# Dilated convolution on one core: two input loads are moved behind output stores, and all transfers go whole

## The chip, the cores and the metric

The kernel runs on one core of a Trainium2 chip. The core has a matrix engine (TensorE, PE in the profile), a vector engine (VectorE, DVE), a scalar engine (ScalarE, ACT), GpSimd (POOL) and SyncE (SP). In this kernel SP computes nothing: it issues every DMA, the transfers between HBM and the on-chip memory SBUF. The metric is the device time of one execution in microseconds (us). The profile is of one execution; its span runs from the first to the last instruction.

## The reference

A 3x3 convolution with dilation 2 and padding 2 over 16 images of 64 channels and 64 x 64 pixels, to 128 output channels:

```python
batch, c_in, h, w, c_out, k, dilation = 16, 64, 64, 64, 128, 3, 2
for b in range(batch):
    for co in range(c_out):
        for ci in range(c_in):
            for kh in range(k):
                for kw in range(k):
                    output[b, co] += weight[co, ci, kh, kw] * x_pad[b, ci, kh*dilation:kh*dilation+h, kw*dilation:kw*dilation+w]
```

Input and output are float32. The input is 16.8 MB, the output 33.6 MB, so two bytes are stored for each byte that is loaded.

## The kernel before

**Pairs and groups.** Two images share the 128 partitions (64 channels each), which makes 8 pairs, 0 to 7. Each pair is worked in 4 groups of 16 output rows, so that the main loop runs over 32 groups G = 0 to 31; pair 0 is G 0 to 3, pair 6 is G 24 to 27, pair 7 is G 28 to 31.

**One group.** PE makes three sums in PSUM: psP from the row sums xs, then psA and psB from the f16 input. psP has one buffer, psA and psB share three. ACT copies psP to SBUF (p_sb, L261). DVE adds p_sb to psA and to psB and writes the result into the output ring osb (L268). The next group's psP cannot be started before ACT has copied the last one out.

**Input.** A pair is loaded as float32 into one of three x32 buffers (L65, in the function load) and then cast to f16 in four chunks by ACT (L83) or POOL (L85). The f16 tiles have four buffers. Which chunk is cast in which group stands in a table, CASTS; chunk c belongs to pair c // 4. In group G, ACT runs the p_sb copy first and the casts of the table behind it. The entries that matter here are these:

```python
12: ((24, A), (25, A)),
13: ((26, A), (27, A)),
16: ((28, A), (29, A)),
17: ((30, A), (31, A)),
```

Chunks 24 to 27 are pair 6 and are needed by the matmuls from G = 24 on; chunks 28 to 31 are pair 7 and are needed from G = 28 on. ACT runs its instructions in the order of the program.

**Output.** The ring osb holds the outputs of three pairs (12.6 MB). Pair 3 writes the place of pair 0, pair 4 that of pair 1, and so on.

**The order of the transfers.** All DMAs are issued by SP, in the order of the program; the schedule is written by hand. Before the loop come the weights, pair 0 in two parts, pair 1 and pair 2. Pairs 3, 4 and 5 are loaded at the ends of G = 0, 2 and 3, when an x32 buffer comes free. At G = 5 and 6 the table MIXED issues pairs 6 and 7 in halves of 1 MB, each half followed by a half of one image of pair 0 (half_load, L223, and store, L206). From G = 7 on each pair is stored when its last group is done: pairs 1 and 2 in halves of images, pairs 3 to 6 as whole images of 2 MB. The last pair is stored twice, after its second and its fourth group. In all SP issues 38 DMAs.

Of the kernel before, what the change touches and what calls it, by code (L numbers as in the profile page):

```python
# [10 lines left out]
def kernel(  # L11
# [7 lines left out]
    nc = tc.nc  # L19

    B, CI, H, W = x.shape
# [7 lines left out]
    P = 128  # L29
    f32 = mybir.dt.float32  # L30
# [4 lines left out]
    HW = H * W  # L35
    GR = 16
    NG = H // GR
# [9 lines left out]
    fpool = ctx.enter_context(tc.tile_pool(name="fpool", bufs=XF))  # L47
# [7 lines left out]
    x_pair = x.rearrange("(nb two) c h w -> nb (two c) (h w)", two=2)  # L55
# [4 lines left out]
    x32_tiles, x16_tiles, xs_tiles = {}, {}, {}  # L60

    def load(pb, cuts=(0, H)):
        x32_tiles[pb] = fpool.tile([P, HW], f32, tag="x32", name="x32")
        for lo, hi in zip(cuts[:-1], cuts[1:]):
            nc.sync.dma_start(  # L65
                out=x32_tiles[pb][:, lo * W : hi * W], in_=x_pair[pb, :, lo * W : hi * W]
            )
# [3 lines left out]
    def o_pair(pb):  # L71
        at = pb % OB * 2 * HW
        return o_ring[:, at : at + 2 * HW]
# [13 lines left out]
    def rowsum(c):  # L87
        pb, g = divmod(c, NG)
        if g == 0:
            xs_tiles[pb] = sxpool.tile([P, HW // 2], f16, tag="xs", name="xs")  # L90
        v = x16_tiles[pb][:, g * GR * W : (g + 1) * GR * W].rearrange(
            "p (b e q) -> p b e q", e=2, q=2 * W
        )
        s = xs_tiles[pb][:, g * NH : (g + 1) * NH].rearrange("p (b q) -> p b q", q=2 * W)
        nc.vector.tensor_tensor(out=s, in0=v[:, :, 0], in1=v[:, :, 1], op=add)  # L95
# [33 lines left out]
    def turn(k):  # L129
# [24 lines left out]
        out=x16_tiles[0][:, 8 * W : 18 * W], in_=x32_tiles[0][:, 8 * W : 18 * W]  # L154
# [23 lines left out]
    def casts(G):  # L178
        for c, eng in CASTS.get(G, ()):
            cast(c, eng)  # L180

    def product(ps, src, kind, blk0, nblk, first, last):
        for j in (1, 0, 2):
            dw = (j - 1) * d
            o0, o1 = max(0, -dw), W - max(0, dw)
            t = kind * KW + j
            for hb in range(2):
                pp = slice(hb * CI, (hb + 1) * CI)
                rhs = src(pp, dw + o0, dw + o1)
                po = ps[:, hb * NH + blk0 * 2 * W : hb * NH + (blk0 + nblk) * 2 * W]  # L190
                po = po.rearrange("p (r w) -> p r w", w=W)[:, :, o0:o1]
                nc.tensor.matmul(  # L192
                    out=po,
                    lhsT=w_sb[pp, t * CO : (t + 1) * CO],
                    rhs=rhs,
                    start=first and j == 1,
                    stop=last and j == 2,
                )

    def blocks(x16, b0, n, e):  # L200
        v = x16.rearrange("p (b e r w) -> p b e r w", e=2, r=2, w=W)
        return lambda pp, c0, c1: v[pp, b0 : b0 + n, e, :, c0:c1]

    def store(pb, m, r0=0, r1=H, rows=((0, P),)):
        for lo, hi in rows:
            nc.sync.dma_start(  # L206
                out=out_img[2 * pb + m, lo:hi, r0 * W : r1 * W],
                in_=o_pair(pb)[lo:hi, m * HW + r0 * W : m * HW + r1 * W],
            )

    def pair_store(pb):
        cuts = (0, H // 2, H) if pb < 3 else (0, H)
        for lo, hi in zip(cuts[:-1], cuts[1:]):
            for m in range(2):
                store(pb, m, lo, hi)

    LOADS = {0: (3,), 2: (4,), 3: (5,)}

    def half_load(pb, k):
        if k == 0:  # L220
            x32_tiles[pb] = fpool.tile([P, HW], f32, tag="x32", name="x32")
        r = slice(k * HW // 2, (k + 1) * HW // 2)
        nc.sync.dma_start(out=x32_tiles[pb][:, r], in_=x_pair[pb, :, r])  # L223

    MIXED = {5: ((6, 0, 0, 0), (6, 1, 0, 1)), 6: ((7, 0, 1, 0), (7, 1, 1, 1))}
    FOUR = ((0, P - 4), (P - 4, P))
    ROWS4 = 8

    for G in range(ngroups):
        pb, g = divmod(G, NG)  # L230
        x16 = x16_tiles[pb]
        xs = xs_tiles[pb].rearrange("p (r w) -> p r w", w=W)
        o = o_pair(pb).rearrange("p (m b e q) -> p m b e q", m=2, e=2, q=2 * W)
        b0 = g * NBLK

        def summed():
            ps = ppool.tile([P, 2 * NH], f32, tag="p", name="psP")
            sv = lambda pp, c0, c1: xs[pp, g * GR // 2 : (g + 1) * GR // 2, c0:c1]
            product(ps, sv, 0, 0, NBLK, True, True)
            return ps  # L240

        if G:
            psP = summed()

        psA = apool.tile([P, 2 * NH], f32, tag="ab", name="psA")
        product(psA, blocks(x16, b0, NBLK, 1), 1, 0, NBLK, True, False)
        z = 1 if g == 0 else 0
        product(psA, blocks(x16, b0 + z - 1, NBLK - z, 1), 2, z, NBLK - z, False, True)

        psB = apool.tile([P, 2 * NH], f32, tag="ab", name="psB")  # L250
        product(psB, blocks(x16, b0, NBLK, 0), 3, 0, NBLK, True, False)
        z = 1 if g == NG - 1 else 0
        product(psB, blocks(x16, b0 + 1, NBLK - z, 0), 4, 0, NBLK - z, False, True)

        if not G:
            psP = summed()

        if not G:
            casts(0)
        p_sb = spool.tile([P, 2 * NH], f32, tag="psb", name="p_sb")  # L260
        nc.scalar.copy(out=p_sb, in_=psP)  # L261
        if G:
            casts(G)
        if G + 1 < ngroups:
            rowsum(G + 1)
        pv = p_sb.rearrange("p (m b q) -> p m b q", m=2, q=2 * W)
        for e, ps in ((0, psA), (1, psB)):
            nc.vector.tensor_tensor(  # L268
                out=o[:, :, b0 : b0 + NBLK, e],
                in0=ps.rearrange("p (m b q) -> p m b q", m=2, q=2 * W),  # L270
                in1=pv,
                op=add,
            )

        for q in LOADS.get(G, ()):
            load(q)
        for q, k, h, m in MIXED.get(G, ()):
            half_load(q, k)
            store(0, m, h * H // 2, (h + 1) * H // 2)
        if G <= 6:  # L280
            continue
        if pb == npairs - 1:
            if g % 2 == 1:
                store(pb, 0, (g - 1) * GR, (g + 1) * GR)
                if g == 1:
                    store(pb, 1, 0, 2 * GR - ROWS4)
                    store(pb, 1, 2 * GR - ROWS4, 2 * GR, FOUR)
                else:
                    store(pb, 1, (g - 1) * GR, (g + 1) * GR)
        elif g == NG - 1:  # L290
            pair_store(pb)

# [33 lines left out]
```

## Time and profile before

| what | value |
|---|---|
| time, median of 3 runs (lowest to highest) | 127.23 us (127.01 to 127.34) |
| the profiled execution: time, span | 126.86 us, 125.0 us |
| PE busy | 104.9 us (84%) |
| DVE busy | 92.7 us (74%) |
| ACT busy | 58.7 us (47%) |
| HBM read and written | 17.07 MB, 33.55 MB |
| mean DMA rate over the span | 406 GB/s |

The time is 1.86 us more than the span, which is what lies outside the first and the last instruction. A DMA has two times in the trace: when SP issues it, and when it lands, that is when its completion reaches the waiting engine. The time from issue to landing holds the wait behind everything that was issued before it. In the rows of the timeline the first number is the start, the second the length from the first start to the last end, both in us, and xN the number of instructions merged into the row. In the rows of the stretches (windows) the line gives the stretch, then the busy time and the count of each engine, the granted PE clock, the busy share of the DMA engines and GB/s.

### The profile page before, as it was taken

What the parts mean: (1) busy time and instruction counts of PE and PEld (TensorE: products, weight loads), DVE (VectorE), ACT (ScalarE), POOL (GpSimd) and SP (SyncE); (2) the same over time, 40 slices, a digit from 0 to 9 for tenths busy, and PEclk for the clock granted to TensorE, in tenths of its full rate; (3) what the DMA queues carried; (4) which work ended last, traced back from release to release, by engine and by line L of the source; (5) the groups of instructions that cost most, each with busy time, mean ns of one, the idle gap of its engine ahead of it and who ended that gap; (6) DMA issues with size and microseconds to landing.
All of it is one profiled execution on the core that took longest, in us unless ns stands there. A gap on an engine that the chain in (4) does not pass through costs nothing.

```text
span 125.0 us, 2358 instructions
## 1 busy us (share of the span) xinstructions
PE 104.9 (84%) x1000; PEld 55.2 (44%) x1000; DVE 92.7 (74%) x103; ACT 58.7 (47%) x61; POOL 9.6 (8%) x15
## 2 busy tenths in 40 slices
PE   6876999999999999999999999999999999800000
PEld 2343444555555555555555555555555555300000
DVE  0752998989998889879988898889888988720000
ACT  4375876798569437943794333333333333300000
POOL 2402305124200000000000000000000000000000
PEclk9999999999999999999999999999999999996555
DMA  4999999999999999999999999999999999999991
GB/s 128 376 428 445 430 430 435 419 425 425 390 375 422 422 432 422 427 419 419 425 432 427 414 443 435 430 425 430 440 425 419 430 435 425 435 409 415 428 383 68
DMA packets 5330, 50.78 MB, mean 406 GB/s; under 512 B 584, under 2 KB 584, under 8 KB 1096
## 3 DMA queue, kind: packets, MB, share of 16 engines
q1 hardware_dynamic: 5320, 50.63, 96.7%
q8 instruction: 8, 0.13, 0.4%
q14 instruction: 2, 0.02, 0.0%
HBM read 17.07 MB, written 33.55 MB: 405 GB/s over the span
## 4 chain that ended last, share of the span: by engine, by line
PE 69%; DVE 1%; DVEq 1%; issue 0%
PE psA L192 28%; PE psB L192 27%; PE psP L192 14%; DVE osb L268 1%; DVEq L324 1%; DVEq L268 0%
## 5 line engine op out<-in xcount | busy, mean ns | idle before, releaser
L192 PEld LDWEIGHTS <-w_sb 64*128 64x128 f16 x960 | 53.3, 94 | 48.8 <-issue 2.0
L261 ACT COPY p_sb<-psP 128x1024 f32<-128x1024 f32 x32 | 32.4, 1012 | 41.0 <-PE psP L192 39.1
L268 DVE TENSOR_TENSOR osb<-psA,p_sb 128x1024 f32<-128x1024 f32 x32 | 39.1, 1223 | 12.5 <-PE psA L192 6.1
L192 PE MATMUL psA<-x,w_sb 64*128 64x496 f16 (+3 forms) x384 | 45.0, 365 | 0.8 <-ACT x L156 0.8
L192 PE MATMUL psB<-x,w_sb 64*128 64x496 f16 (+3 forms) x384 | 45.0, 365 | 0.0
L268 DVE TENSOR_TENSOR osb<-psB,p_sb 128x1024 f32<-128x1024 f32 x32 | 39.0, 1219 | 0.0
L192 PE MATMUL psP<-xs,w_sb 64*128 64x496 f16 (+1 forms) x192 | 26.0, 371 | 1.7 <-ACT p_sb L261 1.5
L83 ACT CAST x<-x 128x1024 f16<-128x1024 f32 (+2 forms) x24 | 24.3, 1051 | 3.4 <-DMA x<-in_x_dram 3.4
L95 DVE TENSOR_TENSOR xs<-x 128x512 f16<-128x512 f16 x32 | 15.6, 488 | 0.7 <-ACT x L83 0.7
L85 POOL CAST x<-x 128x896 f16<-128x896 f32 (+2 forms) x7 | 7.4, 1067 | 19.3 <-DMA x<-in_x_dram 19.3
L111 PE MATMUL dm<-zero 128*128 128x512 f16 x10 | 4.1, 532 | 1.2 <-DVE zero L103 1.2
L121 DVE CAST wd<-w 128x192 f16<-128x192 f32 x1 | 0.5, 499 | 2.6 <-DMA w<-in_weight_dram 2.6
L111 PEld LDWEIGHTS <-zero 128*128 128x128 f16 x10 | 1.0, 121 | 2.6 <-DVE zero L103 1.2
L134 PEld LDWEIGHTS <-wd 128*64 128x64 f16 x30 | 0.9, 109 | 1.9 <-DVE wd L121 1.3
L134 PE MATMUL wt<-ident,wd 128*64 128x128 f16 x30 | 1.4, 224 | 0.4 <-DVE wd L121 0.4
L123 ACT ACT_TABLE_LOAD x1 | 1.3, 1283 | 0.7 <-PEq L310 0.7
L123 ACT CAST wd<-w 128x192 f16<-128x192 f32 x1 | 0.5, 542 | 1.7 <-DMA w<-in_weight_dram 1.7
L146 ACT CAST w_sb<-wt 128x384 f16<-128x384 f32 x1 | 0.5, 479 | 1.2 <-PE wt L134 1.2
L156 ACT CAST x<-x 128x512 f16<-128x512 f32 x1 | 0.6, 617 | 0.8 <-DMA x<-in_x_dram 0.8
L122 POOL TENSOR_TENSOR wd<-w 128x192 f16<-128x192 f32 x1 | 0.8, 794 | 2.5 <-DMA w<-in_weight_dram 2.5
L153 DVE CAST x<-x 128x640 f16<-128x640 f32 x1 | 0.5, 494 | 0.6 <-DMA x<-in_x_dram 0.6
L103 DVE MEMSET zero<- 128x256 uint32 x1 | 0.3, 272 | 0.9 <-PEq L310 0.9
(12 smaller groups left out, 4.6 us busy)
## 6 DMA issues: line engine op xcount, KB each, us to landing
out_dram<-osb SPq DMA_DIRECT2D x8, 2048.0 KB, 17.9
out_dram<-osb SPq DMA_DIRECT2D x15, 1024.0 KB, 19.6
x<-in_x_dram SPq DMA_DIRECT2D x5, 2048.0 KB, 13.1
x<-in_x_dram SPq DMA_DIRECT2D x4, 1024.0 KB, 15.9
x<-in_x_dram SPq DMA_DIRECT2D x1, 1088.0 KB, 5.6
x<-in_x_dram SPq DMA_DIRECT2D x1, 960.0 KB
out_dram<-osb SPq DMA_DIRECT2D x1, 768.0 KB, 14.8
w<-in_weight_dram SPq DMA_DIRECT2D x1, 288.0 KB, 3.0
```

Source lines behind the costliest of these rows:

```text
L83: eng.copy(out=out, in_=in_)
L85: eng.tensor_copy(out=out, in_=in_)
L95: nc.vector.tensor_tensor(out=s, in0=v[:, :, 0], in1=v[:, :, 1], op=add)
L111: nc.tensor.matmul(out=dm[:, 0:512], lhsT=zero[:, 0:P], rhs=zero)
L122: nc.gpsimd.tensor_tensor(out=wdv[:, 3], in0=wv[:, 0], in1=wv[:, 1], op=sub)
L123: nc.scalar.copy(out=wdv[:, 2], in_=wv[:, 0])
L134: nc.tensor.matmul(out=wts[k % 3][r * CI : (r + 1) * CI, c0 + j * CO : c0 + (j + 1) * CO], lhsT=wd[:, t * CI : (t + 1) * CI], rhs=ident,)
L156: nc.scalar.copy(out=x16_tiles[0][:, 0 : 8 * W], in_=x32_tiles[0][:, 0 : 8 * W])
L192: nc.tensor.matmul(out=po, lhsT=w_sb[pp, t * CO : (t + 1) * CO], rhs=rhs, start=first and j == 1, stop=last and j == 2,)
L261: nc.scalar.copy(out=p_sb, in_=psP)
L268: nc.vector.tensor_tensor(out=o[:, :, b0 : b0 + NBLK, e], in0=ps.rearrange("p (m b q) -> p m b q", m=2, q=2 * W), in1=pv, op=add,)
L324: with _tile.TileContext(nc) as tc:
```

## The change

Pairs 6 and 7 are no longer loaded in halves between the stores of pair 0. They become entries of the table LOADS, at G = 7 and G = 11, and pairs 1 and 2 are stored ahead of that load in their last group. Pair 0 is stored at the end of G = 3, behind the load of pair 5. All stores of pairs 0 to 6 are of whole images. The table CASTS is as it was.

```diff
     def pair_store(pb):
-        cuts = (0, H // 2, H) if pb < 3 else (0, H)
-        for lo, hi in zip(cuts[:-1], cuts[1:]):
-            for m in range(2):
-                store(pb, m, lo, hi)
-
-    LOADS = {0: (3,), 2: (4,), 3: (5,)}
-
-    def half_load(pb, k):
-        if k == 0:
-            x32_tiles[pb] = fpool.tile([P, HW], f32, tag="x32", name="x32")
-        r = slice(k * HW // 2, (k + 1) * HW // 2)
-        nc.sync.dma_start(out=x32_tiles[pb][:, r], in_=x_pair[pb, :, r])
-
-    MIXED = {5: ((6, 0, 0, 0), (6, 1, 0, 1)), 6: ((7, 0, 1, 0), (7, 1, 1, 1))}
+        for m in range(2):
+            store(pb, m)
+
+    LOADS = {0: (3,), 2: (4,), 3: (5,), 7: (6,), 11: (7,)}
...
+        later = pb in (1, 2)
+        if g == NG - 1 and later:
+            pair_store(pb)
         for q in LOADS.get(G, ()):
             load(q)
-        for q, k, h, m in MIXED.get(G, ()):
-            half_load(q, k)
-            store(0, m, h * H // 2, (h + 1) * H // 2)
-        if G <= 6:
-            continue
         if pb == npairs - 1:
...
-        elif g == NG - 1:
+        elif g == NG - 1 and not later:
             pair_store(pb)
```

The order in SP's queue is then: weights, pairs 0 to 5, two images of pair 0, two of pair 1, load of pair 6, two images of pair 2, load of pair 7, and from there on stores alone, 30 DMAs in all.

## The prediction

> **What bounds the kernel now.** I read the page's header and slices first, to see which resource is never idle.
>
> ```profile
> span 125.0 us, 2358 instructions
> PE   6876999999999999999999999999999999800000
> DMA  4999999999999999999999999999999999999991
> ```
>
> Each digit is a fortieth of the span. PE is full up to about 109 us and then has nothing to do; the DMA engines are full from 3 us to the end. So two things run side by side: 50.63 MB through the queue, and 32 groups on PE. The end is the queue's. PE's own end matters only if it moves far enough to let the queue run dry.
>
> Next the stretches, for the rate of the queue and the clock (the last three columns are granted clock, DMA share, GB/s).
>
> ```profile
> 34.50:41.00 6.50, 6.50 (x66) 3.57 (x64) 6.01 (x8) 5.62 (x6) 0.00 (x0) 1.00 0.98 397
> 38.30:56.00 17.70, 17.70 (x174) 9.55 (x171) 15.10 (x18) 11.71 (x13) 0.00 (x0) 1.00 1.01 425
> 60.00:100.00 40.00, 40.00 (x394) 21.81 (x390) 35.66 (x40) 16.94 (x17) 0.00 (x0) 1.00 1.01 429
> 112.00:113.00 1.00, 0.00 (x0) 0.00 (x0) 0.00 (x0) 0.00 (x0) 0.00 (x0) 1.00 0.95 401
> 113.00:114.00 1.00, 0.00 (x0) 0.00 (x0) 0.00 (x0) 0.00 (x0) 0.00 (x0) 0.72 0.96 408
> ```
>
> A mixed queue (38 to 56 us) and a queue of stores (60 to 100 us) move at 425 and 429 GB/s. At 427 a transfer of 2.097 MB takes 4.9 us.
>
> Then the DMA issues, one at a time: issue time from SP's timeline, and size and time to landing from the list of issues.
>
> ```profile
> 23.07 0.33 SPq L65 DMA_DIRECT2D x<-in_x_dram  x1
> x<-in_x_dram SPq DMA_DIRECT2D x1, 2048.0 KB, 11.4
> 28.76 0.33 SPq L223 DMA_DIRECT2D x<-in_x_dram  x1
> x<-in_x_dram SPq DMA_DIRECT2D x1, 1024.0 KB, 9.5
> x<-in_x_dram SPq DMA_DIRECT2D x1, 1024.0 KB, 19.9
> ```
>
> Pair 5 is issued at 23.07 and lands at 34.5. The first half of pair 6 lands at 28.76 + 9.5 = 38.3. The last row is the second half of pair 7, issued at about 33.1 and landed at 53.0: three half stores and three half loads were issued between pair 5 and it, and it came behind all of them. A load waits for the stores issued before it; the queue serves in order of issue.
>
> Last, the timeline around the casts of pairs 6 and 7.
>
> ```profile
> 48.65 2.10 ACT L83 CAST x<-x 128x1152 f16<-128x1152 f32 x2
> 50.75 1.01 ACT L261 COPY p_sb<-psP 128x1024 f32<-128x1024 f32 x1
> 53.03 0.81 PE L192 MATMUL psP<-xs,w_sb 64*128 64x512 f16 x6
> ...
> 61.02 2.10 ACT L83 CAST x<-x 128x1152 f16<-128x1152 f32 x2
> 63.12 1.01 ACT L261 COPY p_sb<-psP 128x1024 f32<-128x1024 f32 x1
> 65.40 0.81 PE L192 MATMUL psP<-xs,w_sb 64*128 64x512 f16 x6
> ```
>
> At 48.65 (G = 12) ACT casts pair 6, and behind it, in ACT's order, stands the p_sb copy of G = 13, which PE needs to start psP of G = 14 at 53.03. At 61.02 (G = 16) it is the same with pair 7, the copy of G = 17, and psP of G = 18 at 65.40. Before the change both pairs have landed by then (latest 53.0).
>
> **The change part by part.** The sum runs against the profiled execution: 126.86 us, of which 125.0 is span and 1.86 lies outside; the median is 0.37 higher.
>
> *Whole transfers.* Twelve half stores become six, four half loads two: 38 DMAs become 30. Bytes stay. Eight issues of 0.34 us go from SP, which lies idle. In the queue, halves land 2.45 us apart (38.3 to 53.0 is six of them), 2 x 2.45 = 4.9, as a whole one takes; so I take nothing. The bounds are 0 and the one place where halves were slow: from 34.5 to 40.74 (the first half store's landing, 29.14 + 11.6) two halves took 6.2 instead of 4.9 us, 1.3 lost as the queue went from loads to stores.
>
> *Pair 0's stores* leave at about 24.5 us, when the group's second add ends (23.23 + 1.22), instead of at 29 to 35, behind pair 5 in the queue; the order of service stays gapless, since pair 1's first store, issued at 38.29 before, can go by then at the latest, and pair 0's 4.19 MB keep the queue busy until 34.5 + 9.8 = 44.3 or later. The first group of pair 3, which overwrites pair 0's place, writes at 48.86; pair 0 has landed by 45.6 at the latest. No new wait there. SP's 22.2 us of waits on landings (11.5 on stores, 10.7 on loads) mostly vanish, worth nothing as the queue was full under them.
>
> *Pair 6's load* is moved behind four images (8.39 MB). From pair 5's landing: 34.5 + 5 x 4.9 = 59.0, or 60.3 if the turn from loads to stores costs 1.3 again. I take 60.3, since the nearest row is that same turn; the two ends are kept. ACT wants it at 48.65, so ACT stands still for 11.7 us. Queued behind on ACT is the copy of G = 13: 60.3 + 2.1 (two casts) = 62.4, copied by 63.4, psP of G = 14 starts at 63.4 instead of 53.0. PE is 10.4 us late. DVE follows, its adds need p_sb; it is busy 2.93 of 3.10 us per group (two adds of 1.22 and a row sum of 0.49), so it wins nothing back.
>
> *Pair 7's load* stands behind two more images: 60.3 + 3 x 4.9 = 75.0 (73.7 without the turn). The queue is full up to there: pair 2 is complete at G = 11, before any delay (about 48.5). ACT comes to G = 16's casts at 61.02 + 10.4 = 71.4 and waits 3.6 us: casts to 77.1, copy of G = 17 to 78.1, psP of G = 18 at 78.1 instead of 65.4. PE is 12.7 us late in total; this second wait contains the first, so 12.7 depends on 75.0 alone.
>
> *The end.* From G = 18 on nothing is loaded and the queue lives on what PE delivers. Pair 3's stores go at 60.77 + 10.4 = 71.2, and behind pair 7 they land at 75.0 + 9.8 = 84.8. Pair 4's go at 73.14 + 12.7 = 85.8: the queue is dry. A cold start costs 2.3 us beyond the bytes: the weights, 0.295 MB, were issued at 0.73 and used at 3.74, 3.0 us less 0.7 for bytes. Pair 4 lands at 85.8 + 2.3 + 9.8 = 97.9, pair 5, issued at 98.2, at 110.3, pair 6 is issued at 97.88 + 12.7 = 110.6, dry again. From there 8.39 MB are left (pairs 6 and 7): 110.6 + 2.3 + 19.6 = 132.5. Pair 7's last stores, issued at 110.25 + 12.7 = 123.0, are queued in time. The tail after the last landing is 1.0 us (124.0 to 125.0 now). Span 133.5, time 135.4; against the median 135.7.
>
> In short: time is about 122.7 + delay above a delay of 4.1 us, from the profile's 126.86 with the span's 125.0 as floor, since below that the queue doesn't run dry.
>
> One page speaks for a longer time: the Trainium skill, "DMA: Bandwidth & Descriptors", section "Specifications", gives an HBM limit per core of about 358 GB/s, below the 435 of the fabric. By it, as an estimate, a whole transfer takes 5.9 us, pair 7 lands 8 x 0.96 = 7.7 us later, the last 8.39 MB take 3.8 us more, and the time is near 147. This trace disagrees: 429 GB/s over 40 us.
>
> **The rivals.**
>
> *Loads don't wait for stores* (faster). If reads overtook queued writes, pair 6 would land soon after its issue at 38 us and pair 7 after its at 49 us, ahead of 48.65 and 61.02; no wait arises, the end stays the queue's, and at best the turn's 1.3 us are saved: 127.2 - 1.3 = 125.9. It decides from the point where the delay falls under 4.1 us, that is where pair 7 lands before 66.4. Against it stands the landing at 53.0 of a load issued at 33.1. 0.04.
>
> *The wait is hidden* (same, 127.2): the same threshold, reached by part of that overtaking. With bytes in order, the queue would have to move 16.8 MB from 34.5 to 66.4, 526 GB/s; no slice of the page shows over 445. 0.03.
>
> *Every turn costs* (slower still). After the change the queue turns three times more (stores to pair 6, to stores, to pair 7). At 1.3 each pair 7 lands at 78.9 and the time is 139.6. For: the turn at 34.5. Against: the alternating halves after it ran at 425 GB/s. 0.10.
>
> *The clock falls* (slower a little). PE stops at 108.9 and its granted clock is 1.00 up to 113 and 0.50 by 114, so some 4.5 us of idling. The first wait (10.4 us) is longer, the second (PE idle 2.3 us) shorter. After the first wait PE starts slow; the six opening dummies took 457 ns each from 1.18 us, the two at 4.59 took 300, so the slow start lasts at most 3.4 us and costs at most 1.7. The second wait, 2.3 us long, hides that. If the clock falls there too, 1.7 show: 137.4. 0.08. The Trainium skill, "TensorE: Matmul & The Clock Gate", part 1, has it that one idle window of about 3.4 us halves the clock and about 3.4 us of work restores it; by that the second wait wouldn't, and the sum stays.
>
> **How the numbers follow.** The forecast as computed has 0.75: 135.7. Its lower end is no turn loss (134.4) with the fastest slice's 445 GB/s (eight transfers 0.19 us shorter each), 132.9. Its upper end takes the clock's 137.4 and a second turn. The range of 133 to 138.5 leaves out the overtaking and hidden cases (0.07) and most of the turns (0.08). A measurement can tell about 0.3% (0.4 us) from no change. Faster 0.04, same 0.03, slower 0.93.
>
> **What would show it.** Right: ACT's waits on input grow from 3.4 us to about 19, one of 11.7 at 48.7 and one of 3.6 at 71.4; PE has holes before G = 14 and G = 18; the DMA slices fall under 9 from about 85 us on; GB/s is unchanged before. Wrong: pair 6 landing before 54 us, or DMA slices full to the end in spite of PE's holes, which would mean that the queue had more in store than I count.

## The result

The changed kernel takes 138.01 us, median of 6 runs (137.52 to 138.16), against 127.28 us of the kernel before in 6 runs. The ratio is 1.082, with a 95% interval from 1.0766 to 1.0873. The forecast was 135.7 us, range 133.0 to 138.5. The profiled execution took 138.06 us, with a span of 136.2 us.

**The page after.** The header and slices of the changed kernel:

```profile
span 136.2 us, 2343 instructions
PE   6896998999999996003999989999999999980000
PEclk9999999999999999955599999999999999999555
DMA  4999999999999999999996996399479929999981
```

PE has a hole in slices 16 to 19 (it stands still from 53.3 to 63.5 us), and its granted clock falls in it. The DMA slices are full until about 72 us and have holes from there to the end: the queue, which was the bound, now runs out of work.

**Who waits.** Lines of the changed kernel's list of waits (engine, line, releaser; us in total, times, longest):

```profile
DVE osb L258 <- ACT p_sb L251: 20.0, 11, 11.8
ACT x L83 <- DMA x<-in_x_dram: 17.4, 6, 11.6
PE psP L192 <- ACT p_sb L251: 12.6, 4, 10.2
```

The middle line is where the loss starts, with 3.4 us before the change: ACT waits for input. The other two follow from it: PE waits for the p_sb copy that stands behind the cast on ACT, and DVE for the same copy.

**The casts of pairs 6 and 7**, in the timeline of the changed kernel:

```profile
60.42 2.10 ACT L83 CAST x<-x 128x1152 f16<-128x1152 f32 x2 [11.62 <-DMA x<-in_x_dram]
62.42 1.00 ACT L251 COPY p_sb<-psP 128x1024 f32<-128x1024 f32 x1
63.48 1.44 PE L192 MATMUL psP<-xs,w_sb 64*128 64x512 f16 x6 [10.22 <-ACT p_sb L251]
...
75.68 2.10 ACT L83 CAST x<-x 128x1152 f16<-128x1152 f32 x2 [2.08 <-DMA x<-in_x_dram]
77.69 1.00 ACT L251 COPY p_sb<-psP 128x1024 f32<-128x1024 f32 x1
78.74 0.81 PE L192 MATMUL psP<-xs,w_sb 64*128 64x512 f16 x6 [0.68 <-ACT p_sb L251]
```

Pair 6 arrives at 60.4 and pair 7 at 75.7, where the forecast had 60.3 and 75.0. The last add of DVE, before the change and after it:

```profile
109.01 1.22 DVE L268 TENSOR_TENSOR osb<-psB,p_sb 128x1024 f32<-128x1024 f32 x1
122.35 1.21 DVE L258 TENSOR_TENSOR osb<-psB,p_sb 128x1024 f32<-128x1024 f32 x1
```

It starts 13.3 us later. This is what is called the delay below.

### The profile page after: what moved, and what is told of

It reads as the page before. It is cut to its first block, busy times and chain, and to the rows that moved or that the text cites. A ratio compares the mean times of both kernels' runs of the same rounds, so it can differ in the third digit from the quotient of the medians.

```text
span 136.2 us, 2343 instructions
## 1 busy us (share of the span) xinstructions
PE 107.9 (79%) x1000; PEld 57.0 (42%) x1000; DVE 90.9 (67%) x103; ACT 58.4 (43%) x61; POOL 9.5 (7%) x15
## 5 line engine op out<-in xcount | busy, mean ns | idle before, releaser
L192 PEld LDWEIGHTS <-w_sb 64*128 64x128 f16 x960 | 54.7, 95 | 59.9 <-issue 16.2
L192 PE MATMUL psA<-x,w_sb 64*128 64x496 f16 (+3 forms) x384 | 46.3, 373 | 0.2 <-ACT x L156 0.2
L192 PE MATMUL psP<-xs,w_sb 64*128 64x496 f16 (+1 forms) x192 | 26.6, 379 | 12.6 <-ACT p_sb L251 12.6
L83 ACT CAST x<-x 128x1024 f16<-128x1024 f32 (+2 forms) x24 | 24.3, 1049 | 17.4 <-DMA x<-in_x_dram 17.4
L95 DVE TENSOR_TENSOR xs<-x 128x512 f16<-128x512 f16 x32 | 13.9, 435 | 0.7 <-ACT x L83 0.7
L111 PE MATMUL dm<-zero 128*128 128x512 f16 x10 | 4.6, 580 | 1.2 <-DVE zero L103 1.2
L148 DVE CAST w_sb<-wt 128x384 f16<-128x384 f32 x1 | 0.6, 558 | 1.1 <-PE wt L134 1.1
L125 POOL CAST wd<-w 128x192 f16<-128x192 f32 x1 | 0.8, 804 | 0.0
```

Source lines behind the costliest of these rows:

```text
L83: eng.copy(out=out, in_=in_)
L111: nc.tensor.matmul(out=dm[:, 0:512], lhsT=zero[:, 0:P], rhs=zero)
L125: nc.gpsimd.tensor_copy(out=wdv[:, 4], in_=wv[:, 2])
L192: nc.tensor.matmul(out=po, lhsT=w_sb[pp, t * CO : (t + 1) * CO], rhs=rhs, start=first and j == 1, stop=last and j == 2,)
```

## The experiments

The theory: the transfers themselves are no slower in the new order; ACT, which works in program order, stands in front of a load that is still in the queue, PE is late by that, and the queue runs dry. The rivals: the order or the whole transfers cost by themselves; each wait adds its own share; the slow start of PE after a wait costs nothing.

### The casts moved to where the data is there

```diff
-        12: ((24, A), (25, A)),
-        13: ((26, A), (27, A)),
-        16: ((28, A), (29, A)),
-        17: ((30, A), (31, A)),
+        16: ((24, A), (25, A)),
+        17: ((26, A), (27, A)),
+        20: ((28, A), (29, A)),
+        21: ((30, A), (31, A)),
```

> The changed kernel with the casts of pairs 6 and 7 moved from G = 12, 13, 16, 17 to G = 16, 17, 20, 21; all transfers as changed. Theory (the loss is ACT standing in front of a load that came too late, nothing else): ACT comes to pair 6 at about 61 us, after its landing at 60.4, so no wait; to pair 7 at about 73.5, a wait of some 2 us and a PE delay of about 1 us, under the 4.1 us from which the queue runs dry. Time 127.0 (126.3 to 127.7), DMA slices full to the end. Rival (the new order or the whole transfers are slow by themselves): 138 still, or well above 129.

Measured: 126.9 us, ratio 0.9986 (0.9957 to 1.0014) to the kernel before. The whole loss is gone with all transfers as changed. Its timeline and one stretch of it, and then the same stretch of the changed kernel:

```profile
60.98 2.10 ACT L83 CAST x<-x 128x1152 f16<-128x1152 f32 x2
75.28 2.10 ACT L83 CAST x<-x 128x1152 f16<-128x1152 f32 x2 [1.82 <-DMA x<-in_x_dram]
85.00:120.00 35.00, 24.44 (x238) 13.11 (x234) 22.65 (x24) 8.10 (x8) 0.00 (x0) 0.88 1.00 425
```

```profile
85.00:120.00 35.00, 35.00 (x342) 19.31 (x340) 31.20 (x35) 11.22 (x12) 0.00 (x0) 1.00 0.80 338
```

Pair 7 lands within 0.4 us of where it does in the changed kernel (75.3 and 75.7), so the late landing is harmless in itself. What differs is who stands in front of it. With the casts late the queue moves 425 GB/s from 85 to 120 us; in the changed kernel it moves 338 GB/s and is busy for 0.80 of that time. The rival that the order or the whole transfers cost by themselves falls for this order.

### Only one of the two waits

Two kernels leave one wait each. In the first, pair 6 is loaded early and pair 7 stays where the change put it:

```diff
-    LOADS = {0: (3,), 2: (4,), 3: (5,), 7: (6,), 11: (7,)}
+    LOADS = {0: (3,), 2: (4,), 3: (5,), 5: (6,), 11: (7,)}
...
+        if G == 5:
+            load(6)
+            pair_store(0)
+            continue
```

(and pair 0 is no longer stored at G = 3).

> The changed kernel with pair 6 alone loaded early (at G = 5, ahead of pair 0's stores, which follow it); pair 7 has the same bytes in front of it as in the changed kernel and lands at about 75.5. Theory (pair 7's landing alone sets the total delay, the wait for pair 6 is contained in it): ACT waits some 14.5 us once, from 61 us, the delay of PE is 13.4 us as before, and a slow start of the clock of about 2 us comes on top, since no second wait hides it: 140.0 (138.0 to 141.0). Rival (each wait brings its own share): the first one's 10.4 us are gone, 127.6 to 130.5.

Measured: 139.66 us, ratio 1.0982 (1.0955 to 1.1008). Taking the larger of the two waits away makes the kernel 1.65 us slower than the changed kernel.

```profile
75.29 2.10 ACT L83 CAST x<-x 128x1152 f16<-128x1152 f32 x2 [13.75 <-DMA x<-in_x_dram]
78.35 1.44 PE L192 MATMUL psP<-xs,w_sb 64*128 64x512 f16 x6 [12.35 <-ACT p_sb L251]
```

Pair 7's landing alone sets where PE goes on, 78.35 here and 78.74 in the changed kernel; the wait for pair 6 lies inside it. (Storing pair 0 later also makes pair 3's first add wait 1.95 us for its place in the ring; this too lies inside.) The rival that waits add up is out by 9 us. The extra time is the slow start of PE, which comes behind the last wait here: G = 18 takes 5.4 us (78.35 to 83.75) instead of 3.2. In the second kernel pair 7 goes right behind pair 6:

```diff
-    LOADS = {0: (3,), 2: (4,), 3: (5,), 7: (6,), 11: (7,)}
+    LOADS = {0: (3,), 2: (4,), 3: (5,), 7: (6, 7)}
```

> The changed kernel with pair 7 loaded right behind pair 6, ahead of pair 2's stores: it lands at about 65.3, before ACT wants it (73.6). Only the wait for pair 6 is left: 10.4 us. If the slow start of PE after the wait (2 us in the changed kernel, G = 14 taking 5.2 instead of 3.2 us) now shows in full: delay 12.5, 137.2 (136.5 to 137.8). Rival (the slow start costs nothing at the end, only landings count): delay 10.4, 135.1.

Measured: 137.11 us, ratio 1.0806 (1.0749 to 1.0862). The wait for pair 7 is gone, and at most 0.9 us with it: the medians differ by that much, but the interval overlaps that of the changed kernel, and the profiled execution, the slowest of the four, took 138.29 us. What took the wait's place is the slow start of PE. The starts of psP of G = 14 and G = 15 in this kernel:

```profile
63.93 1.44 PE L192 MATMUL psP<-xs,w_sb 64*128 64x512 f16 x6 [10.32 <-ACT p_sb L251]
69.83 0.81 PE L192 MATMUL psP<-xs,w_sb 64*128 64x512 f16 x6
```

G = 14 starts 10.9 us later than before the change (53.03) and takes 5.9 us instead of 3.2; the two together are the 13.6 us by which this execution's last add is late. The stretches of the changed kernel around its first wait (the third number from the end is the granted clock):

```profile
54.00:56.00 2.00, 0.00 (x0) 0.00 (x0) 0.00 (x0) 0.00 (x0) 0.00 (x0) 1.00 0.98 418
56.00:58.00 2.00, 0.00 (x0) 0.00 (x0) 0.00 (x0) 0.00 (x0) 0.00 (x0) 0.85 0.98 418
64.00:66.00 2.00, 2.00 (x14) 0.80 (x12) 2.00 (x3) 2.00 (x3) 0.00 (x0) 0.50 0.98 418
66.00:68.00 2.00, 2.00 (x14) 0.87 (x12) 0.62 (x2) 0.12 (x1) 0.00 (x0) 0.59 1.07 451
...
72.00:74.00 2.00, 2.00 (x24) 1.11 (x22) 1.84 (x4) 1.01 (x1) 0.00 (x0) 1.00 0.29 123
```

PE stops at 53.3. The clock falls to half at about 57.4 (a mean of 0.85 over 56 to 58), PE goes on at 63.5, and the clock is back at about 67.6. Group 14 lasts from 63.48 to 68.69, 5.2 us instead of 3.2: 2.0 us lost. In the changed kernel the wait for pair 7 hides them, since PE comes to it later and waits 0.68 us instead of some 2.7 (0.68 + 2.0, an estimate). Without that wait they stay on the path. (The last row, where the queue is nearly dry, is taken up below.)

### A delay in between

```diff
-        20: ((28, A), (29, A)),
-        21: ((30, A), (31, A)),
+        18: ((28, A), (29, A)),
+        19: ((30, A), (31, A)),
```

(against the kernel with the late casts).

> As the kernel with the late casts, but pair 7's casts at G = 18 and 19 instead of 20 and 21: ACT comes to them at 67.3 and waits some 8 us for the landing at 75.3. Theory: the copy of G = 19 ends at about 78.4, psP of G = 20 starts there instead of at 71.6, 6.8 us late; PE has idled some 6.5 us, the clock falls, and the slow start adds 2 us that nothing hides: delay 8.8, 4.5 less than the changed kernel's 13.3, so 133.5 (132.8 to 134.5). Without the slow start 131.5. If the end didn't follow the delay one to one above the threshold of 4.1 us: 127 or 138.

Measured: 133.26 us, ratio 1.0474 (1.0426 to 1.0522).

```profile
74.99 2.10 ACT L83 CAST x<-x 128x1152 f16<-128x1152 f32 x2 [6.69 <-DMA x<-in_x_dram]
78.05 1.44 PE L192 MATMUL psP<-xs,w_sb 64*128 64x512 f16 x6 [5.29 <-ACT p_sb L251]
```

ACT's wait is a good half of the longest one in the changed kernel (6.69 against 11.62 us), and so is the loss (6.0 against 10.7 us).

### The size of the transfers alone

The kernel before, in its old order, with whole images and whole loads:

```diff
-        cuts = (0, H // 2, H) if pb < 3 else (0, H)
+        cuts = (0, H)
...
-    MIXED = {5: ((6, 0, 0, 0), (6, 1, 0, 1)), 6: ((7, 0, 1, 0), (7, 1, 1, 1))}
+    MIXED = {5: ((6, 0),), 6: ((7, 1),)}
...
-        for q, k, h, m in MIXED.get(G, ()):
-            half_load(q, k)
-            store(0, m, h * H // 2, (h + 1) * H // 2)
+        for q, m in MIXED.get(G, ()):
+            load(q)
+            store(0, m)
```

> The kernel before with the size alone changed: pair 6 whole, an image of pair 0, pair 7 whole, the other image of pair 0 at G = 5 and 6, and pairs 1 and 2 as whole images. Theory: same bytes, loads ahead of need, 127.2 (126.5 to 127.8). Rival (whole transfers hold up the queue or release places in the ring too late): part of the 11 us shows, above 129.

Measured: 131.39 us, ratio 1.0359 (1.0285 to 1.0433). The theory missed this one. The timeline says why:

```profile
55.82 1.23 DVE L268 TENSOR_TENSOR osb<-psA,p_sb 128x1024 f32<-128x1024 f32 x1 [7.04 <-DMA out_dram<-osb]
57.10 2.69 PE L192 MATMUL psB<-x,w_sb 64*128 64x512 f16 x12 [5.08 <-DVE osb L268]
```

DVE's add of G = 12 (pair 3) writes the place of pair 0 in the output ring, both images at once. Whole, the second image of pair 0 is the last of the four transfers and lands at 55.8. Behind that wait the granted clock falls here too: it is at half from about 56.2 to 63.1. In the kernel before, the first halves of both images had landed by 45.7, and the second ones were needed only at G = 14, where its one such wait is 0.8 us:

```profile
55.59 1.22 DVE L268 TENSOR_TENSOR osb<-psA,p_sb 128x1024 f32<-128x1024 f32 x1 [0.78 <-DMA out_dram<-osb]
```

What the halves bring is an early free place in the ring, not speed in the queue. To test this, both images of pair 0 go ahead of pair 7's load:

```diff
-    MIXED = {5: ((6, 0),), 6: ((7, 1),)}
+    MIXED = {5: ((6, (0, 1)),), 6: ((7, ()),)}
...
-        for q, m in MIXED.get(G, ()):
+        for q, ms in MIXED.get(G, ()):
             load(q)
-            store(0, m)
+            for m in ms:
+                store(0, m)
```

> The kernel with whole transfers in the old order, with both images of pair 0 stored ahead of pair 7's load. Theory (what made whole transfers cost 4 us was that pair 0's second image landed at 55.8, and pair 3's first group, which writes the same place in the ring, waited 7.0 us for it): now it lands one transfer earlier, at about 50.9, the wait is about 2 us, under the threshold: 127.1 (126.5 to 127.8). Rival (whole transfers cost by their size): 131 still.

Measured: 127.69 us, ratio 1.0041 (1.0008 to 1.0074). One transfer's place brings 3.7 of the 4.1 us back (medians), so the size itself costs next to nothing. The first add of pair 3 waits 2.31 us now. A second wait was not expected: the first add of pair 4, which writes the place of pair 1, starts at 66.03 after 3.82 us, since pair 1 now stands behind pair 7's load with whole images. It is the same rule one pair on. The last add is still 3.4 us late (112.39 instead of 109.01), which leaves a few tenths.

### The small pieces at the end

```diff
-                if g == 1:
-                    store(pb, 1, 0, 2 * GR - ROWS4)
-                    store(pb, 1, 2 * GR - ROWS4, 2 * GR, FOUR)
-                else:
-                    store(pb, 1, (g - 1) * GR, (g + 1) * GR)
+                store(pb, 1, (g - 1) * GR, (g + 1) * GR)
```

This is made once to the changed kernel and once to the kernel with the late casts.

> The changed kernel with the last pair's second image stored as one piece after G = 29 (1 MB in place of 768, 248 and 8 KB). Theory: the small pieces cost about 0.9 us of rate where they now run alone (127 to 130 us at 291 to 377 GB/s in the changed kernel): 137.1 (136.8 to 137.4). Rival (the end's slow stretch has nothing to do with the pieces): 138.0 or more.

> The kernel with the late casts and the last pair's piece stored whole. Here the queue is full to the end, so the pieces lie among other work: 126.9 as with the late casts (126.4 to 127.5). If the pieces cost also in a full queue: 126.0. If they even out the end of the 16 DMA engines: above 127.5.

Measured: 136.64 us for the first, 1.4 us under the changed kernel and a little under the expected range (ratio to before 1.0727, 1.0688 to 1.0766), and 127.56 us for the second, 0.7 above the late casts and just outside its expected range (ratio to before 1.0019, 0.9999 to 1.0040). One stretch of the changed kernel, and the same stretch without the pieces:

```profile
126.00:130.00 4.00, 0.00 (x0) 0.00 (x0) 0.00 (x0) 0.00 (x0) 0.00 (x0) 0.50 1.00 331
```

```profile
126.00:130.00 4.00, 0.00 (x0) 0.00 (x0) 0.00 (x0) 0.00 (x0) 0.00 (x0) 0.64 1.01 428
```

In the changed kernel the queue runs dry before the last two pairs and moves only 331 GB/s in the stretch with the pieces, with the DMA engines as busy as ever. In a queue that is full to the end the pieces cost nothing that these runs show. Whether they save time there stays open: the medians say 0.7 us, but the intervals of the two ratios overlap (0.9957 to 1.0014 with the pieces, 0.9999 to 1.0040 without). Why they are slow is not shown either; no run shows the DMA engines one by one.

## Why the prediction was right

**The bound.** Right. The end is the queue's until it runs dry, and PE's delay counts from there. The profiled executions of the five kernels whose queue ran dry and that store the small pieces lie on one line. The delay is the start of the last add less 109.01:

| kernel | delay of the last add, us | profiled time, us | time less delay |
|---|---|---|---|
| casts at 18 | 8.5 | 133.15 | 124.6 |
| whole, old order | 8.3 | 132.87 | 124.6 |
| the change | 13.3 | 138.06 | 124.7 |
| pair 7 behind pair 6 | 13.6 | 138.29 | 124.7 |
| pair 6 early | 15.2 | 139.68 | 124.5 |

The form of the forecast's line, a floor and then a slope of one, is confirmed over two ways of delaying PE, a late load in front of ACT (at three places) and a late store in front of DVE. Its constant was 122.7 and is 124.6. So the threshold isn't 4.1 us: with the floor at 126.9, it is 2.3. The kernel with the ring freed early agrees, with a delay of 3.4 us and a profiled time of 128.33, where the line gives 128.0; this is one execution, and the median of its runs is 127.69. With a delay of 0.6 us the late casts lie on the floor. The changed kernel without the small pieces lies below the line: a delay of 13.2 us and a profiled time of 136.67, so a constant of 123.5. The constant thus depends on how the last pair is stored.

**The landings.** Right. The 1.3 us that were counted once, at the turn from loads to stores, came, but one transfer earlier: pair 4's load landed at 29.8, pair 5's at 36.0 and pair 0's first image at 40.9. Pair 5, worked out for 34.5, was 6.3 us behind pair 4 instead of 4.9, and the first store 4.9 behind pair 5. In both kernels it is the load right ahead of the first store that lands late (before the change the first half of pair 6, 3.8 us behind pair 5 instead of 2.45); why is not shown. Pair 7 came 0.7 us later than worked out. Turns that cost 1.3 each would have put it at 78.9; that rival is out. So is the one that loads overtake stores. The issue of pair 6's load and its time to landing:

```profile
37.56 0.84 SPq L65 DMA_DIRECT2D x<-in_x_dram  x1
x<-in_x_dram SPq DMA_DIRECT2D x1, 2048.0 KB, 22.8
```

By the Trainium skill, "DMA: Bandwidth & Descriptors", section "Queues, rings and completion order", each DMA engine takes descriptors in the order of its ring; the landings here agree, in spacing and order: pair 6 lands 24.4 us, or five transfers of 4.9, behind pair 5 (36.0 to 60.4).

**Pair 0's stores, the ring.** Right for the change: pair 0 lands at 45.8 and no add waits. But the paragraph on whole transfers priced them by the queue alone, "I take nothing". In the old order they cost 4.1 us by way of the ring. The change escapes that since it stores pair 0 before any later load; the forecast was right here for a reason it stated only for the new order.

**The clock.** The mechanism was right, the second wait hid the slow start. Its size was off: the slow start was to last at most 3.4 us and cost at most 1.7; it lasted 4.2 us (63.5 to 67.6) and cost 2.0 in the changed kernel. The bound was read from the opening dummies, where the granted clock reads 1.00 in the record; what slowed those is not shown. Part of the second wait was meant to be left, 0.6 us, and 0.68 was. A consequence was overlooked: pair 3's stores, due at G = 15, were themselves 2 us later for it (73.25 instead of 71.2), so that the queue was dry for the first time at 72 to 74 us (the last row of the stretches above, 0.29 busy), and not only after 85. It cost nothing, as pair 4's stores (86.5) come later than pair 3's landing (85.0) in any case. ACT's waits on input came to 17.4 us instead of about 19, since the second one was 2.08 us instead of 3.6: the slow start had brought ACT to these casts later (73.6 instead of 71.4).

**The sum.** It was made for the profiled execution, and there 2.7 us were missing (138.06 against 135.4; for the medians 2.3, 138.0 against 135.7). Of these, 0.6 is the delay (13.3 instead of 12.7), and 2.1 are the term of the last 8.39 MB, put at 2.3 + 19.6 us from pair 6's issue to the last landing. Issued at 111.22, they landed at 135.2 (the last store, issued at 124.00, takes 11.2 us), 24.0 us instead of 21.9. The failed step is the rate of 427 GB/s from the middle of the kernel, applied to the end. It holds for the first half: pair 6's second image had landed by 122.7, 11.5 us after the first issue, where 12.1 were allowed for. The last 4.19 MB, pair 7, then took 12.5 us instead of 9.8. Without the small pieces the same stretch took 11.3 (122.5 to 133.8), so they account for 1.2 us. The other 1.5 us, of which the first half gives 0.6 back, come without them too: there the rate falls to 156, 25 and 8 GB/s from 131 to 134 us, and the sum had no such fall. What causes it is not shown.

That 138.0 lies inside the range is in part luck. The room above 135.7 was meant for a clock that falls at the second wait and for a second turn. Neither came, and the slower end filled that room.

## What to carry to other kernels

A load that lands late costs nothing until an engine that works in order stands in front of it; look for what is queued behind the first consumer (here a copy that PE needs) and move the consumer as well as the load. When the queue is the bound, as here, a delay of compute is free up to the slack and costs one to one beyond it. The slack hangs on the rate of the end, which here was lower than in the middle; read it from the last 10 us. Before a transfer is made larger, look who waits for its place and not only for its speed.

## What the runs showed that was not expected

- Taking away the larger of two waits (11.6 us on ACT) made the kernel slower by 1.65 us: the later wait then held PE for the whole time, and the slow start of PE behind it lay on the path.
- After a wait the granted clock stayed at half for 4.2 us of work in the changed kernel (63.5 to 67.6) and for 5.5 us with pair 7 behind pair 6 (63.9 to about 69.5); G = 14 took 5.2 and 5.9 us instead of 3.2. The Trainium skill, "TensorE: Matmul & The Clock Gate", part 1, has the full clock come back after at least one busy window, about 3.4 us of sustained work; these two runs show more than 3.4. In that second kernel:

```profile
66.00:68.00 2.00, 2.00 (x12) 0.86 (x10) 0.62 (x3) 0.57 (x1) 0.00 (x0) 0.50 0.96 410
68.00:70.00 2.00, 2.00 (x14) 0.92 (x12) 1.21 (x1) 0.00 (x0) 0.00 (x0) 0.63 0.98 410
```

- The same small pieces cost 1.4 us at the end of a queue that runs dry, and nothing that these runs show at the end of one that is full.
- No version beat the kernel before: with the late casts the order of the change gives the same time, and in both kernels the queue is full to the end (425 GB/s from 85 to 120 us with the late casts).
